# Stick-breaking prompt scores as 64-row products, two heads side by side, on one Trainium2 core

## The chip, the cores and the metric

The kernel runs on one core of a Trainium2 chip. The metric is the time of one execution on the device in microseconds (us), the median of several runs; lower is better. The engines are TensorE (matmuls and transposes; PE, its weight loads PEld), VectorE (DVE), ScalarE (ACT), GpSimd (POOL) and SyncE (SP, which issues the DMAs). They run at once, each through its own list of instructions in order, and wait for one another by semaphores.

## What is computed

Two layers of a hybrid encoder over 2048 prompt tokens and 8 x 16 sample tokens, width 1024: an input projection, a state-space branch, a stick-breaking attention branch of 8 heads of 64, and an output projection. The change touches the attention of the prompt alone:

```python
def stick_breaking(q, k, v, q_pos, k_pos):
    z = jnp.einsum('bqhd,bkhd->bhqk', q, k, preferred_element_type=jnp.float32) * (HEAD_DIM ** -0.5)
    mask = k_pos[None, :] < q_pos[:, None]
    log_1mb = jnp.where(mask, -jax.nn.softplus(z), 0.0)
    after = lax.cumsum(log_1mb, axis=3, reverse=True) - log_1mb
    a = jnp.where(mask, jnp.exp(jax.nn.log_sigmoid(z) + after), 0.0)
    return jnp.einsum('bhqk,bkhd->bqhd', a.astype(v.dtype), v)
```

## The kernel before

Q and K lie in DRAM transposed (`qT`, `kT`), each value split into a high part and a low part (`[512, 2, SEQ]`: 8 heads of 64 rows, two parts, tokens), since the matmuls take them at reduced precision.

`attn_prompt` (L778) runs over blocks of up to four query tiles of 128 tokens and over four pairs of heads (L782), then over key chunks of 512 tokens, the diagonal one first (L800), the two heads `hh` (L807) and the query tiles `i`. For one head, K's 64 rows of high and 64 of low parts fill all 128 rows of the array (`K1`); Q is loaded twice, as `Q1` in the same arrangement and as `Q2` with the parts exchanged. One score tile `pz` (128 queries x 512 keys, one PSUM bank) is then the sum of two products, L819 and L820, which hold all four combinations of parts. On the diagonal chunk the mask is added by a third product (L822), and a tile that needs less than 256 columns is computed at 256.

ScalarE turns `pz` into `u`, the sigmoid of minus the score (L824). VectorE multiplies `u` up from the right with a scan, in place (L826). TensorE transposes 128 columns of `u` of each query tile into `pt` (L836), VectorE copies the first head's `pt` to SBUF (L838) and ScalarE the second's (L839), and two products, one for each head on 64 of the array's columns, add `aT` times the differences of V into `po` (L842). At the end of a head pair VectorE adds a last term and multiplies by the gate (L851).

PSUM has eight banks. Until the last projection of layer 1 they are dealt out as two `m` (projections), two `z` (scores, but also parts of the state-space branch, of the sample attention and of the modulation), one `r` (`pr`: the transposes of the norm, L634, and of q and k, L696), two `t` and one `o`. After that, for the attention of layer 1, they are one `m`, three `z`, three `t` and one `o` (L109). Tiles with one tag take that tag's buffers in turn, in the order in which the program text asks for them.

The order on each engine is not the order of the program text: a scheduler puts ready instructions of later stages among those of earlier ones. In layer 0, the program text calls `attn_prompt(0)`, `glu(0)`, the modulation, `output(0, 0)` and then the projections of layer 1; on the engines these stages overlap.

Other lines that are spoken of: L673 to L675 and L726 to L728 (input projections), L1241 to L1243 (output projection), L1049 (transposes of 64 rows in the state-space branch), L242 (modulation, on 32 of the array's columns).

Of the kernel before, what the change touches and what calls it, by code (L numbers as in the profile page):

```python
# [8 lines left out]
F32 = mybir.dt.float32  # L9
F32R = mybir.dt.float32r  # L10
BF16 = mybir.dt.bfloat16
AF = mybir.ActivationFunctionType
# [32 lines left out]
class Trunk:  # L45
# [6 lines left out]
    def build(self):  # L52
        tc, nc = self.tc, self.nc
        with ExitStack() as es:
            self.dram = es.enter_context(tc.tile_pool(name="dram", bufs=1, space=DRAM))
            self.cp = self.pool(es, "const")
            self.pes = ExitStack()
            self.mb, self.zb, self.tb, self.ob = 2, 2, 2, 1
            self.ps = self.pes.enter_context(tc.tile_pool(name="ps", bufs=1, space=PSUM))
            self.scratch()  # L60
            self.consts()
            with ExitStack() as pe:
                with ExitStack() as px:
                    self.xp, self.xf = self.pool(px, "xp", right=True), []
                    self.rs0 = self.xp.tile([128, NT], F32, name="rs")
                    self.fetch(0)
                    self.fetch(1)
                    with ExitStack() as pv:
                        su = self.pool(pv, "sv", right=True)
                        self.mod(0, (2, 3, 0, 1))  # L70
                        self.ssm_params(su)
                    st = self.proj_open(pe, 0, 0)
                    with tc.high_priority(offset=300):
                        self.project(st, ("u",))
                self.project(st, ('q',))
                with ExitStack() as pq:
                    self.stats(self.pool(pq, "stats1", right=True), TILES[1])
                self.ssm_mats(0)
                with ExitStack() as ph:
                    self.ssm_phase(ph, 0)  # L80
                    self.ssm_phase(ph, 1)
                self.ssm_mats(1)
                self.ssm_sample(0)
                self.project(st, ('k', 'v', 'za', 'zs'))
                self.proj_half(st, 1)
                self.project(st, ("u",))
                self.ssm(0)
                self.attn_sample(0)
                self.project(st, ('zs', 'za', 'k', 'v', 'q'))
            self.attn_prompt(0, ((0, 4), (4, 4), (8, 4), (12, 4)))  # L90
            self.glu(0)
            self.mod(0, (4, 5), right=False)
            self.mod(1, (2, 3, 0, 1, 4, 5), right=False)
            self.output(0, 0)
            with ExitStack() as pe:
                st = self.proj_open(pe, 1, 0)
                self.project(st, ("u",))
                self.project(st, ('q', 'k', 'v', 'za', 'zs'))
            self.attn_sample(1)
            self.output(0, 1)  # L100
            with ExitStack() as pe:
                st = self.proj_open(pe, 1, 1)
                self.project(st, ("u",))
                self.ssm_sample(1)
                self.ssm(1)
                self.project(st, ('k', 'v', 'q', 'zs', 'za'))
            self.pes.close()
            self.ps = es.enter_context(tc.tile_pool(name="ps2", bufs=1, space=PSUM))
            self.mb, self.zb, self.tb, self.ob = 1, 3, 3, 1  # L109
            self.attn_prompt(1, ((0, 4), (4, 4), (8, 4)) + ((12, 2), (14, 2)))  # L110
            self.glu(1)
            self.output(1, 0)
            self.output(1, 1)
# [61 lines left out]
        return self.ps.tile([128, 512], F32, name="pm", tag="m", bufs=self.mb)  # L175

    def pr(self):
        return self.ps.tile([128, 512], F32, name="pr", tag="r", bufs=1)

    def po(self):  # L180
        return self.ps.tile([128, 512], F32, name="po", tag="o", bufs=self.ob)
# [595 lines left out]
    def attn_prompt(self, l, blocks):  # L777
        nc = self.nc  # L778
        v, gp, sc, pe, ident = nc.vector, nc.gpsimd, nc.scalar, nc.tensor, self.ident
        with ExitStack() as es:  # L780
            ap = self.pool(es, f"a{l}{blocks[0][0]}", right=True)
            for t0, nt, hp in [(t0, nt, hp) for t0, nt in blocks for hp in range(H // 2)]:  # L782
                nq = nt * 128
                qs = slice(t0 * 128, t0 * 128 + nq)
                rp = slice(hp * 128, (hp + 1) * 128)
                top = (t0 + nt - 1) // 4
                Qt = []
                for hh in range(2):
                    rs = slice(hp * 128 + hh * 64, hp * 128 + hh * 64 + 64)
                    Q1 = ap.tile([128, 512], F32R, name="Q1", bufs=3)  # L790
                    Q2 = ap.tile([128, 512], F32R, name="Q2", bufs=3)
                    self.dma(Q1[:, 0:nq], self.qT[l][rs, :, qs].rearrange("d s t -> (d s) t"))
                    self.dma(Q2[:, 0:nq], self.qT[l][rs, ::-1, qs])
                    Qt.append((Q1, Q2))
                po = self.po()
                vE = ap.tile([128, 4], F32, name="vE", bufs=2)
                with nc.allow_non_contiguous_dma(reason="layout"):
# [2 lines left out]
                for kc in range(top, -1, -1):  # L800
                    diag = kc == top
                    nk = (t0 + nt) * 128 - kc * 512 if diag else 512
                    ks = slice(kc * 512, kc * 512 + nk)
                    V1 = ap.tile([128, 4, 128], F32, name="V1", bufs=2)
                    self.dma(V1[:, 0:nk // 128], self.dv_d[l][ks, rp].rearrange("(b p) c -> p b c", p=128))
                    As = [[], []]
                    for hh in range(2):  # L807
                        rs = slice(hp * 128 + hh * 64, hp * 128 + hh * 64 + 64)
                        K1 = ap.tile([128, 512], F32R, name="K1", bufs=3)
                        self.dma(K1[:, 0:nk], self.kT[l][rs, :, ks].rearrange("d s t -> (d s) t"))  # L810
                        Q1, Q2 = Qt[hh]
                        for i in range(nt):
                            W = (t0 + i + 1) * 128 - kc * 512 if diag else 512
                            o = 512 - W
                            pz = self.pz()
                            qi = slice(i * 128, (i + 1) * 128)
                            N = max(W, 256)
                            c0, c1 = 512 - N, 512 - N + W
                            pe.matmul(pz[:, c0:512], Q1[:, qi], K1[:, 0:N], start=True, stop=False)  # L819
                            pe.matmul(pz[:, c0:512], Q2[:, qi], K1[:, 0:N], start=False, stop=not diag)  # L820
                            if diag:
                                pe.matmul(pz[:, c1 - 128:c1], self.identb, self.maskb, start=False, stop=True)  # L822
                            u = ap.tile([128, 512], F32, name="u", bufs=16)
                            sc.activation(u[:, o:512], pz[:, c0:c1], AF.Sigmoid, scale=-0.125)  # L824
                            un = u[:, o:512][:, ::-1]
                            v.tensor_tensor_scan(un, un, un, 1.0 if diag else carry[hh * 4 + i], ALU.mult, ALU.bypass)  # L826
                            carry[hh * 4 + i] = u[:, o:o + 1]
                            As[hh].append(u)
                    for j in range(nk // 128):
                        i0 = max(0, kc * 4 + j - t0)  # L830
                        s = slice(i0 * 128, nq)
                        pTs = [self.pt(), self.pt()]
                        for hh in range(2):
                            for i in range(i0, nt):
                                off = (512 - ((t0 + i + 1) * 128 - kc * 512)) if diag else 0
                                pe.transpose(pTs[hh][:, i * 128:(i + 1) * 128], As[hh][i][:, off + j * 128:off + (j + 1) * 128], ident)  # L836
                        aTs = [ap.tile([128, 512], F32, name="aT", bufs=4) for _ in range(2)]
                        v.tensor_copy(aTs[0][:, s], pTs[0][:, s])  # L838
                        last = sc.copy(aTs[1][:, s], pTs[1][:, s])  # L839
                        for hh in range(2):  # L840
                            c = slice(hh * 64, hh * 64 + 64)
                            mm = pe.matmul(po[c, s], V1[:, j, c], aTs[hh][:, s], start=diag and j == 0,  # L842
                                           stop=kc == 0 and j == 3, tile_position=(0, hh * 64))
                            if hh == 0:
                                self.after(mm, last)
# [436 lines left out]
```

## Time and profile before

| | |
|---|---|
| median of 3 runs | 3268.61 us (3263.9 to 3268.92) |
| the profiled execution | 3266.1 us, span 3264.3 us |
| VectorE busy | 2228.8 us |
| ScalarE busy | 1297.2 us |
| chain that ended last | TensorE 24%, VectorE 3% of the span, the rest under 2% each |
| score products L819 | from 1031.7 to 3212.5 us |

All times that are worked out stand beside the profiled execution's 3266.1 us. A matmul's duration in the profile includes a tail in which the next one already runs, so what a matmul holds of TensorE is read from the starts of neighbours, in the timeline.

### The profile page before, as it was taken

The numbers are of one execution on the slowest core, as the hardware profiler recorded it, in microseconds if no ns is written. First come the engines' busy times: TensorE is split into PE (matmuls) and PEld (weight loads), VectorE is DVE, ScalarE is ACT, GpSimd is POOL, SyncE is SP. The second block draws the span as 40 slices with busy tenths as digits, with TensorE's granted clock in tenths as the row PEclk, the third lists the DMA queues.
The fourth block names the chain that finished last, engine by engine and source line by source line (L and its number), as shares of the span: only waits on it lengthen the run. The fifth ranks groups of instructions, "written<-read, shape, count | busy, mean of one in ns | idle before, by whom it ended". The sixth has DMA issues, their size and how long they took to land. (4 is left out here: it accounts for less than half of the span.)

```text
span 3264.3 us, 47172 instructions
## 1 busy us (share of the span) xinstructions
PE 3019.6 (93%) x16902; PEld 2241.4 (69%) x16902; DVE 2228.8 (68%) x3885; ACT 1297.2 (40%) x2646; POOL 715.0 (22%) x468
## 2 busy tenths in 40 slices
PE   6978679899998999999999999989999899999998
PEld 4756577798767667667777785757789565666665
DVE  6699785667466776677895534376583989776865
ACT  5622225334342343465443324263343345343422
POOL 1155663102211022211021002222200202111210
PEclk8989899999999999999999999999999899999999
DMA  6645654565776974343344237437853846444642
GB/s 208 164 141 176 215 166 150 146 192 167 258 241 216 315 218 151 121 139 117 113 150 153 88 104 268 142 99 216 268 177 119 259 129 200 141 128 136 203 140 73
DMA packets 516100, 555.28 MB, mean 170 GB/s; under 512 B 87203, under 2 KB 369491, under 8 KB 515098
## 3 DMA queue, kind: packets, MB, share of 16 engines
q1 hardware_dynamic: 515866, 552.26, 53.9%
q8 instruction: 134, 2.20, 0.3%
q14 instruction: 100, 0.82, 0.1%
HBM read 378.12 MB, written 169.86 MB: 168 GB/s over the span
## 5 line engine op out<-in xcount | busy, mean ns | idle before, releaser
L826 DVE TENSOR_TENSOR_SCAN u<-u 128x512 f32<-128x512 f32 (+3 forms) x640 | 722.2, 1162 | 94.2 <-ACT u L824 90.7
L673 PE MATMUL pm<-wH,hH 128*128 128x512 f32 x1088 | 448.9, 414 | 38.4 <-ACT kn L760 18.9
L675 PE MATMUL pm<-wH,hL 128*128 128x512 f32 x1088 | 446.2, 410 | 10.6 <-POOL hL L649 6.0
L674 PE MATMUL pm<-wL,hH 128*128 128x512 f32 x1088 | 444.0, 408 | 9.9 <-DVE wL L172 8.0
L839 ACT COPY aT<-pt 128x512 f32<-128x512 f32 (+1 forms) x376 | 174.9, 469 | 595.3 <-PE pt L836 569.1
L836 PEld LDWEIGHTS pt<-ident,u 128*128 128x128 f32 x2176 | 242.1, 142 | 230.8 <-issue 194.1
L824 ACT ACTIVATE u<-pz 128x512 f32<-128x512 f32 (+3 forms) x640 | 320.7, 535 | 177.1 <-PE pz L822 61.3
L838 DVE COPY aT<-pt 128x512 f32<-128x512 f32 (+1 forms) x376 | 199.4, 533 | 253.8 <-PE pt L836 242.3
L836 PE MATMUL pt<-ident,u 128*128 128x128 f32 x2176 | 352.0, 285 | 12.9 <-DVE aT L838 9.3
L842 PE MATMUL po<-aT,V 128*64 128x512 f32 (+1 forms) x1504 | 317.7, 505 | 16.0 <-DVE aT L838 8.1
L819 PE MATMUL pz<-K,Q 128*128 128x512 f32 (+2 forms) x640 | 272.9, 427 | 6.1 <-ACT u L824 1.8
L726 PE MATMUL pm<-hH,wH 128*128 128x384 f32 (+1 forms) x768 | 258.9, 337 | 18.4 <-DVE kn L731 18.4
L673 PEld LDWEIGHTS pm<-wH,hH 128*128 128x128 f32 x1088 | 210.0, 193 | 90.2 <-ACT kn L760 20.4
L728 PE MATMUL pm<-hH,wL 128*128 128x384 f32 (+1 forms) x768 | 257.4, 336 | 10.2 <-POOL wL L172 10.2
L172 POOL TENSOR_TENSOR wL<-wr,wH 128x512 fp32r<-128x512 f32 x96 | 152.1, 1595 | 498.2 <-ACT wH L171 326.8
L727 PE MATMUL pm<-hL,wH 128*128 128x384 f32 (+1 forms) x768 | 257.8, 336 | 0.0
L675 PEld LDWEIGHTS pm<-wH,hL 128*128 128x128 f32 x1088 | 210.2, 193 | 66.2 <-POOL hL L649 10.6
L674 PEld LDWEIGHTS pm<-wL,hH 128*128 128x128 f32 x1088 | 210.2, 193 | 58.8 <-DVE wL L172 11.3
L820 PE MATMUL pz<-K,Q 128*128 128x512 f32 (+2 forms) x640 | 236.3, 370 | 0.0
L1241 PE MATMUL pm<-owH,mH 128*128 128x512 f32 x512 | 205.0, 402 | 2.1 <-ACT mH L171 1.2
L1242 PE MATMUL pm<-owL,mH 128*128 128x512 f32 x512 | 204.1, 399 | 3.1 <-DVE owL L172 3.1
L1243 PE MATMUL pm<-owH,mL 128*128 128x512 f32 x512 | 202.4, 396 | 0.0
(373 smaller groups left out, 5252.0 us busy)
## 6 DMA issues: line engine op xcount, KB each, us to landing
wr<-in_w_in_dram SPq DMA_DIRECT2D x192, 256.0 KB
K<-kT SPq DMA_DIRECT2D x184, 256.0 KB
Q<-qT SPq DMA_DIRECT2D x112, 256.0 KB
wm<-in_w_mod_dram SPq DMA_DIRECT2D x24, 1024.0 KB
V<-dv_d SPq DMA_DIRECT2D x92, 256.0 KB
out_dram<-kn SPq DMA_DIRECT2D x68, 256.0 KB
qT<-x SPq DMA_DIRECT2D x64, 256.0 KB
kT<-x SPq DMA_DIRECT2D x64, 256.0 KB
```

The costliest lines, as they stand in the source:

```text
L673: pe.matmul(ps, hH[:, k, cs], wH[k], start=k == 0, stop=False)
L674: pe.matmul(ps, hH[:, k, cs], wL[k], start=False, stop=False)
L675: pe.matmul(ps, hL[:, k, cs], wH[k], start=False, stop=k == KT - 1)
L726: pe.matmul(ps[:, 0:n], wH[k][:, ws], hH[:, k, 0:n], start=k == 0, stop=False)
L727: pe.matmul(ps[:, 0:n], wH[k][:, ws], hL[:, k, 0:n], start=False, stop=False)
L728: pe.matmul(ps[:, 0:n], wL[k][:, ws], hH[:, k, 0:n], start=False, stop=k == KT - 1)
L819: pe.matmul(pz[:, c0:512], Q1[:, qi], K1[:, 0:N], start=True, stop=False)
L820: pe.matmul(pz[:, c0:512], Q2[:, qi], K1[:, 0:N], start=False, stop=not diag)
L824: sc.activation(u[:, o:512], pz[:, c0:c1], AF.Sigmoid, scale=-0.125)
L826: v.tensor_tensor_scan(un, un, un, 1.0 if diag else carry[hh * 4 + i], ALU.mult, ALU.bypass)
L836: pe.transpose(pTs[hh][:, i * 128:(i + 1) * 128], As[hh][i][:, off + j * 128:off + (j + 1) * 128], ident)
L842: mm = pe.matmul(po[c, s], V1[:, j, c], aTs[hh][:, s], start=diag and j == 0, stop=kc == 0 and j == 3, tile_position=(0, hh * 64))
```

## The change

Q and K are now loaded once for both heads, with head 0 in rows 0 to 63 and head 1 in rows 64 to 127 and the two parts side by side (`Q`, `K`, 128 x 2 x 512). A score tile is the sum of three products of 64 rows: high by high, low by high, high by low; low by low is left out. The products of the two heads alternate, each on its 64 rows of the array (`tile_position=(hh * 64, 0)`), into two `pz` tiles. The first of the six also waits for an earlier sigmoid, so that both tiles are free. The tag `r` is gone: `pr` takes its buffers from the tag `z`, which has three instead of two.

```diff
-            self.mb, self.zb, self.tb, self.ob = 2, 2, 2, 1
+            self.mb, self.zb, self.tb, self.ob = 2, 3, 2, 1
...
     def pr(self):
-        return self.ps.tile([128, 512], F32, name="pr", tag="r", bufs=1)
+        return self.ps.tile([128, 512], F32, name="pr", tag="z", bufs=self.zb)
...
+            free = []
...
-                Qt = []
-                for hh in range(2):
-                    rs = slice(hp * 128 + hh * 64, hp * 128 + hh * 64 + 64)
-                    Q1 = ap.tile([128, 512], F32R, name="Q1", bufs=3)
-                    Q2 = ap.tile([128, 512], F32R, name="Q2", bufs=3)
-                    self.dma(Q1[:, 0:nq], self.qT[l][rs, :, qs].rearrange("d s t -> (d s) t"))
-                    self.dma(Q2[:, 0:nq], self.qT[l][rs, ::-1, qs])
-                    Qt.append((Q1, Q2))
+                Q = ap.tile([128, 2, 512], F32R, name="Q", bufs=2)
+                self.dma(Q[:, :, 0:nq], self.qT[l][rp, :, qs])
...
+                    K = ap.tile([128, 2, 512], F32R, name="K", bufs=3)
+                    self.dma(K[:, :, 0:nk], self.kT[l][rp, :, ks])
                     As = [[], []]
-                    for hh in range(2):
-                        rs = slice(hp * 128 + hh * 64, hp * 128 + hh * 64 + 64)
-                        K1 = ap.tile([128, 512], F32R, name="K1", bufs=3)
-                        self.dma(K1[:, 0:nk], self.kT[l][rs, :, ks].rearrange("d s t -> (d s) t"))
-                        Q1, Q2 = Qt[hh]
-                        for i in range(nt):
...
-                            pe.matmul(pz[:, c0:512], Q1[:, qi], K1[:, 0:N], start=True, stop=False)
-                            pe.matmul(pz[:, c0:512], Q2[:, qi], K1[:, 0:N], start=False, stop=not diag)
+                    for i in range(nt):
...
+                        pzs = [self.pz(), self.pz()]
+                        for n, (a, b) in enumerate(((0, 0), (1, 0), (0, 1))):
+                            for hh in range(2):
+                                r = slice(hh * 64, hh * 64 + 64)
+                                mm = pe.matmul(pzs[hh][:, c0:512], Q[r, a, qi], K[r, b, 0:N], start=n == 0,
+                                               stop=n == 2 and not diag, tile_position=(hh * 64, 0))
+                                if n == 0 and hh == 0 and len(free) >= self.zb - 1:
+                                    self.after(mm, free[1 - self.zb])
+                        for hh in range(2):
+                            pz = pzs[hh]
...
-                            sc.activation(u[:, o:512], pz[:, c0:c1], AF.Sigmoid, scale=-0.125)
+                            free.append(sc.activation(u[:, o:512], pz[:, c0:c1], AF.Sigmoid, scale=-0.125))
```

In the changed kernel the lines of `attn_prompt` below the products stand one higher: L814 is a score product, L821 the mask, L835 a transpose, L841 a value product.

The scheduler makes another order of the whole program from it. The first place is TensorE's list late in layer 0's attention before: score products beside transposes (L836), value products (L842) and the first norm transposes of layer 1 (L634).

```order
L819 MATMUL pz<-K_11510,Q_11383 128x512 [waits Activation_49]
L820 MATMUL pz<-K_11510,Q_11384 128x512
L819 MATMUL pz<-K_11510,Q_11383 128x512 [waits Activation_49]
L820 MATMUL pz<-K_11510,Q_11384 128x512
L836 MATMUL pt<-ident,u 128x128 [waits DVE_49]
L836 MATMUL pt<-ident,u 128x128 x2
L836 MATMUL pt<-ident,u 128x128 [waits Activation_49]
L836 MATMUL pt<-ident,u 128x128 x2
L634 MATMUL pr<-ident,x_15654 128x128 [waits Activation_49]
L634 MATMUL pr<-ident,x_15654 128x128 x3
```

Scores, transposes of `u` and the norm's transposes all use the whole array here, and the first norm of layer 1 stands among scores of layer 0; more of these follow behind it.

The second place is TensorE's list in the changed kernel at the end of layer 0's scores.

```order
L841 MATMUL po<-aT,V_13952 64x512 [waits DMAHW5_49,Activation_49]
L841 MATMUL po<-aT,V_13952 64x512
L835 MATMUL pt<-ident,u 128x128 [waits PE_49]
L835 MATMUL pt<-ident,u 128x128 x3
L814 MATMUL pz<-K,Q 128x512 [waits Activation_49]
L814 MATMUL pz<-K,Q 128x512 x5
L634 MATMUL pr<-ident,x_15798 128x128 [waits Activation_49]
L634 MATMUL pr<-ident,x_15798 128x128 x3
L835 MATMUL pt<-ident,u 128x128 [waits DVE_49]
L835 MATMUL pt<-ident,u 128x128 x3
```

The six products L814 stand between rows of the whole array, and the L634 shown is the first one of layer 1: it follows the last score group of layer 0. Ahead of it, back to the last output projection, the list holds only rows like these.

## Rows read from the trace of the kernel before

**Rows 1.** Page, busy time, share of the span and instructions of each engine.

```profile
PE 3019.6 (93%) x16902; PEld 2241.4 (69%) x16902; DVE 2228.8 (68%) x3885; ACT 1297.2 (40%) x2646; POOL 715.0 (22%) x468
```

**Rows 2.** Stretches: us, busy of PE, PEld, DVE, ACT, POOL; PEclk, DMA, GB/s.

```profile
1600.00:1900.00 300.00, 297.83 (x1560) 218.72 (x1559) 210.17 (x353) 120.24 (x223) 50.61 (x33) 1.00 0.38 123
...
2700.00:2800.00 100.00, 95.25 (x504) 60.04 (x502) 87.38 (x101) 49.00 (x99) 23.88 (x14) 0.98 0.68 204
...
2224.00:2475.00 251.00, 246.28 (x1298) 204.81 (x1298) 176.89 (x420) 102.93 (x207) 41.95 (x32) 1.00 0.66 201
```

**Rows 3.** Groups by line and shape, attention: busy us, mean ns | idle before.

```profile
L819 PE MATMUL pz<-K,Q 128*128 128x512 f32 x448 | 200.5, 447 | 3.2 <-DMA K<-kT 1.7 <-ACT u L824 1.4
...
L819 PE MATMUL pz<-K,Q 128*128 128x384 f32 x64 | 26.7, 417 | 0.0
...
L819 PE MATMUL pz<-K,Q 128*128 128x256 f32 x128 | 45.8, 358 | 2.9 <-issue 1.6 <-DVE kn L731 0.9 <-ACT u L824 0.4
...
L826 DVE TENSOR_TENSOR_SCAN u<-u 128x512 f32<-128x512 f32 x448 | 587.4, 1341 | 62.6 <-ACT u L824 59.8
...
L838 DVE COPY aT<-pt 128x512 f32<-128x512 f32 x172 | 117.6, 684 | 156.8 <-PE pt L836 155.3 <-PE po L842 0.7
...
L842 PE MATMUL po<-aT,V 128*64 128x256 f32 x560 | 90.9, 408 | 11.2 <-DVE aT L838 8.1 <-issue 2.9 <-DVE za L851 0.2
...
L851 DVE SCALAR_TENSOR_TENSOR za<-po,vE,za 128x128 f32<-128x128 f32 x126 | 35.2, 337 | 11.1 <-PE po L842 10.9
```

**Rows 4.** Timeline of PE and PEld near 3102 us: start, us, engine, line.

```profile
3101.45 0.48 PE L819 MATMUL pz<-K,Q 128*128 128x512 f32 x1
3101.77 0.39 PE L820 MATMUL pz<-K,Q 128*128 128x512 f32 x1
3102.00 0.38 PE L836 MATMUL pt<-ident,u 128*128 128x128 f32 x2
3102.31 0.65 PE L842 MATMUL po<-aT,V 128*64 128x256 f32 x4
3102.89 0.44 PE L836 MATMUL pt<-ident,u 128*128 128x128 f32 x2
...
3101.53 0.19 PEld L820 LDWEIGHTS pz<-K,Q 128*128 128x128 f32 x1
```

**Rows 5.** Timeline of PE and PEld near 2315 us; last, one L1049 load by shape.

```profile
2314.47 0.40 PE L675 MATMUL pm<-wH,hL 128*128 128x512 f32 x1
2314.80 1.21 PE L1049 MATMUL pt<-ident,y 64*128 64x64 f32 x16
2315.93 0.50 PE L673 MATMUL pm<-wH,hH 128*128 128x512 f32 x1
2316.27 0.40 PE L674 MATMUL pm<-wL,hH 128*128 128x512 f32 x1
...
2315.47 0.39 PEld L1049 LDWEIGHTS pt<-ident,y 64*128 64x128 f32 x5
...
L1049 PEld LDWEIGHTS pt<-ident,y 64*128 64x128 f32 x256 | 17.1, 139 | 4.7 <-issue 3.0 <-DVE xs L1010 0.6 <-ACT wH L171 0.4
```

**Rows 6.** L824 by shape; L836's durations (ns, min/median/max) by its line.

```profile
L824 ACT ACTIVATE u<-pz 128x512 f32<-128x512 f32 x448 | 250.5, 599 | 117.3 <-PE pz L820 60.7 <-PE pt L836 35.6 <-PE pz L822 15.3
...
L836 PE MATMUL pt<-ident,u x2176: 270/273/476, 1035.2 to 3249.0; 128*128 128x128 f32 x198
```

**Rows 7.** Who waited for whom, PE: us in total, times, longest us.

```profile
PE pr L696 <- DVE x L707: 18.8, 7, 10.6
...
PE pr L634 <- ACT x L639: 6.0, 6, 2.5
...
PE pz L819 <- ACT u L824: 1.8, 4, 1.2
...
PE pz L819 <- DMA K<-kT: 1.7, 1, 1.7
```

More of the change, by code (lines that the diff above doesn't have):

```diff
@@ L805, in attn_prompt @@
                     self.dma(V1[:, 0:nk // 128], self.dv_d[l][ks, rp].rearrange("(b p) c -> p b c", p=128))
+                    K = ap.tile([128, 2, 512], F32R, name="K", bufs=3)
+                    self.dma(K[:, :, 0:nk], self.kT[l][rp, :, ks])
                     As = [[], []]
-                    for hh in range(2):
-                        rs = slice(hp * 128 + hh * 64, hp * 128 + hh * 64 + 64)
-                        K1 = ap.tile([128, 512], F32R, name="K1", bufs=3)
-                        self.dma(K1[:, 0:nk], self.kT[l][rs, :, ks].rearrange("d s t -> (d s) t"))
-                        Q1, Q2 = Qt[hh]
-                        for i in range(nt):
[L813 to L818, printed above, removed]
-                            pe.matmul(pz[:, c0:512], Q1[:, qi], K1[:, 0:N], start=True, stop=False)
-                            pe.matmul(pz[:, c0:512], Q2[:, qi], K1[:, 0:N], start=False, stop=not diag)
+                    for i in range(nt):
+                        W = (t0 + i + 1) * 128 - kc * 512 if diag else 512
+                        o = 512 - W
+                        qi = slice(i * 128, (i + 1) * 128)
+                        N = max(W, 256)
+                        c0, c1 = 512 - N, 512 - N + W
+                        pzs = [self.pz(), self.pz()]
[8 more added lines that the diff above has]
+                            pz = pzs[hh]
                             if diag:
```

## The prediction, made before the changed kernel ran

> **What bounds the kernel now.** I read the page's busy times first. TensorE is busy 93% of the 3264.3 us span, VectorE 68% [rows 1], so the average points at TensorE. Then the same by stretch, since the change touches only the attention on the prompt: late in layer 0's attention TensorE is busy 297.83 of 300 us, VectorE 210.17; in layer 1's attention 95.25 and 87.38 of 100 [rows 2]. TensorE sets the pace in both, but only because the scheduler mixes attention with projections. Attention alone asks more of VectorE: a scan of 512 columns takes 1341 ns and there are two for each query tile and head pair, and one copy of 684 ns for every 128 keys of the four query tiles of a block [rows 3]. So two questions decide: what the new score products cost TensorE, and whether the mixing survives.
>
> **The products saved.** A 512-column score product holds TensorE 0.23 us (from L820's start at 3101.77 to the next at 3102.00) [rows 4]; its busy time of some 0.4 us includes a tail that the next product overlaps. Per head pair and query tile there were four products; now there are three steps of two 64-row products each. If the two of a step run side by side, one step of 0.23 us is saved. By the counts of L819 [rows 3], two heads together: 224 x 0.23 + 32 x 0.17 + 64 x 0.12 = 52 + 5 + 8 = 65 us (the narrower steps scaled by columns). That two products side by side do run at the price of one is shown on the column halves: four L842 products of 256 columns begin and end in 0.65 us [rows 4], where one alone is busy 408 ns [rows 3]. Bounds: 65 us saved, or, if nothing overlaps, 130 us lost (six steps for four); I take the saving, by that nearest row.
> The Trainium skill, "TensorE: Matmul & The Clock Gate", Part 3, gives 3.07 times for four row tiles of 512 columns, 77% of ideal; by that a step would be an estimated 0.30 us and the sum 47 us worse. No run here shows row tiles side by side yet.
>
> **The change of array shape.** All score products used the full array, like the transposes and projections around them. Now a group of six stands in 64-row tiles, between others in the full array. Before shows what such an excursion costs: L1049's transposes use 64 rows. From L675's start at 2314.47 to L674's at 2316.27 is 1.80 us [rows 5]. In it stand L675 and L673 (0.23 each) and 16 transposes, whose step is 0.062 us: five weight loads span 0.39, one is 139 ns, so (0.39 - 0.14) / 4. That makes 1.45; 0.35 us is over, 0.175 a change of shape. Part is a pause (L675 holds 0.33 rather than 0.23), part the first weight load, which no product hides (L673 holds 0.34). Counted along TensorE's whole list, changes of shape go from 990 to 1667: 677 more, at 0.175 us 118 us. Bounds: 0.10 us each if the first load hides, 0.20 if two loads at the start stand one behind the other; 68 to 135 us. So the rearranged products cost 118 - 65 = 53 us more than they save. A fifth of the groups (64 of 320, layer 0's last block) go to the stretch below, so this term is 43 us.
>
> **The shared PSUM ring.** `pr` (projection transposes) now takes its buffers in turn with `pz`. In the order of before, layer 1's first norm transposes stand among layer 0's scores; now the first stands behind the very last score. Between the last output projection and that row lie 62 score groups, nearly the whole last block, with nothing beside them but transposes and value products. VectorE's work there, for one head pair: three full key chunks of 8 scans and 4 copies, 3 x (8 x 1.34 + 4 x 0.68) = 40.4 us; the diagonal one, whose widths add up to 2.5 times 512 columns, 2.5 x (2 x 1.34 + 0.68) = 8.4 us; four closings of 0.34 [rows 3]: 50.2 us, 201 for four pairs. TensorE's for the same in before: scores 13.6, 116 transposes of 0.11, value products about 15 with their changes of shape (0.58 for 256 columns, twice the stream about 1.0 for 512) [rows 4, 6]: 43 us, 172 in all, and there it was the bound. At the 87% to 100% that VectorE could reach (87.38 of 100 is the highest row in attention), the stretch takes 201 to 231 us; I take 90%, 223: 51 us lost. Bounds 29 and 59 by this arithmetic; 0 if the order runs better mixed than it reads.
> The same ring pulls apart the sample attention of layer 0 from the q and k projections behind it, and layer 1's state-space scan from its k and q. Each has some 400 rows with few neighbours now; before, TensorE was busy 246.28 of 251 us around the latter, VectorE 176.89 [rows 2]. At the same share lost (51 of 223) of some 110 us, my estimate for 400 rows of 0.11 to 0.23 and the like: 25 us, bounds 0 and 70.
>
> **What gets better, and the added wait.** `pr` had one buffer. TensorE's waits for its release total 18.8 and 6.0 us [rows 7]; two more buffers may remove them: between 0 and -25, I take -14 us, since VectorE's queue, which ends the larger, is late anyway. The first product of a group now waits for the first sigmoid of the group ahead; queued behind it are all later TensorE instructions. A 512-column sigmoid takes 599 ns [rows 6], about 0.8 us from the last product. In the new order 24 of 319 groups come within 1 us of the one ahead, by the steps above: at most 24 x 0.8 = 19 us, probably 4 us; score products lost 1.8 us in such waits before [rows 7]. Q's loads fall to a quarter in number and K's to half on SP's queue; K's bytes are the same, Q's halve. TensorE lost 1.7 us waiting for K [rows 7], so this is 0, and without that cover those 1.7 us.
>
> **Sum.** 43 + 51 + 25 - 14 + 4 = 109 us on the profiled execution's 3266.1 us: 3375 us. That execution lies 2.5 us under the median shown and inside the three runs.
>
> **Rivals.**
> *The mixing is not lost* (0.2): TensorE stays the bound in the long stretch since its own waits shrink. The ring terms fall away, all 53 us of shape changes count, less 10: 3309. For it: TensorE was 95.25 busy where VectorE was 87.38 [rows 2]. Against: 50 us of VectorE stand to 43 of TensorE.
> *Weight loads are no longer hidden inside a group* (0.13). In before it is hidden: L820's load runs from 3101.53 for 0.19 us, while L819 works in the same rows [rows 4]. If the loads of steps two and three wait for their own rows, each exposes what L673 shows after a change, 0.11 us: 320 x 2 x 0.11 = 70, less the fifth that VectorE covers, 56: 3431.
> The Trainium skill, "TensorE: Matmul & The Clock Gate", Part 3, "The mechanism", says that a load overlaps running products only when the row group differs; by that rule this rival would hold. The trace of full-array products disagrees with it.
> *The row tiles do not run side by side* (0.06): six steps, 195 us from the first term, less a fifth, on top: 3531.
> *Faster* (0.08): the shape change is nearly free for these groups, the mechanism of the opposite sign. It decides at 65 / 677 = 0.096 us a change if nothing else were lost. At 0.03 us (20 us), with 20 us of lost mixing and all 25 of `pr`'s waits gone: 3266 - 65 + 20 + 20 - 25 = 3216. Against it are both excursions seen: the column tiles also pause, two transposes of 0.11 and the pause filling 0.31 us ahead of L842 [rows 4, 6].
> *No change* (0.03): the same at 0.08 us a change.
>
> **How the numbers follow.** The forecast has 0.5. The range 3290 to 3445 takes in the first two rivals and the bounds of the ring terms; outside are the faster and unchanged cases, the serial one and a few per cent of tails. Its own case spans 3330 to 3420. About 0.2% (6.5 us) is what a measurement of this kernel can tell from no change: faster 0.08, within 0.04, slower 0.88.
>
> **What would show it.** Steps: L814 in pairs that start together, three steps of 0.23 us a group. Shape: about 0.1 us pause ahead of a group and behind it. Ring: a stretch of some 220 us without projections, VectorE near 90% and TensorE clearly under its 99%, then projections with VectorE idle. Right for the wrong reason would be products of a group 0.2 us apart each. I am wrong if layer 0's attention stays TensorE-bound, or if the pauses are missing.

## The result, and the profile after

The changed kernel is slower: 3635.03 us median of four runs (3631.12 to 3641.03), beside 3266.26 for the kernel before on the same chip. The ratio is 1.1134, with a 95% interval of 1.111 to 1.1159: 369 us more. The forecast was 3375 us, with a range up to 3445: the sign is right, the size is wrong by more than a factor of three (369 against 109).

The page of the changed kernel: busy times, then TensorE's share and clock in 40 slices of the 3639.2 us span.

```profile
PE 3122.9 (86%) x17542; PEld 2227.6 (61%) x17542; DVE 2203.7 (61%) x3885; ACT 1301.3 (36%) x2646; POOL 693.8 (19%) x468
...
PE   6960369999788999999999999894589899999999
...
PEclk8985589999898999999999999897799899999999
```

TensorE is now busy 86% of the span instead of 93% [rows 1]. Its busy time grew by 103 us, the span by 375: most of the loss is a TensorE that stands or runs slowly, and it does so in two places that hold few or no prompt scores, slices 3 to 6 (182 to 546 us) and slices 28 and 29 (2456 to 2638 us).

I divide both programs at layer 0's first score product, its last, and layer 1's first and last. Windows of the changed kernel (us, busy of PE, PEld, DVE, ACT, POOL, clock, DMA, GB/s), first up to the first score, then layer 0's scores, then up to layer 1's, then layer 1's:

```profile
0.00:1164.00 1164.00, 856.75 (x4824) 687.88 (x4824) 668.01 (x1460) 390.39 (x783) 312.49 (x212) 0.86 0.50 156
1164.00:1834.00 670.00, 641.50 (x3935) 382.80 (x3936) 521.82 (x672) 279.78 (x555) 84.12 (x44) 0.96 0.48 150
1834.00:2875.00 1041.00, 899.93 (x4690) 720.22 (x4686) 458.06 (x1045) 344.82 (x685) 177.36 (x142) 0.92 0.45 144
2875.00:3591.00 716.00, 683.38 (x3874) 409.71 (x3874) 538.32 (x679) 277.30 (x601) 114.28 (x66) 0.97 0.47 146
```

The same four in the kernel before:

```profile
0.00:1032.00 1032.00, 882.77 (x5008) 712.10 (x5008) 726.31 (x1493) 395.92 (x798) 341.24 (x217) 0.95 0.60 187
1032.00:1887.00 855.00, 838.37 (x4719) 588.22 (x4719) 602.78 (x987) 373.77 (x733) 131.38 (x82) 0.99 0.49 157
1887.00:2524.00 637.00, 602.52 (x3406) 476.52 (x3404) 338.41 (x697) 241.74 (x491) 123.38 (x99) 0.98 0.56 176
2524.00:3212.00 688.00, 651.85 (x3548) 436.12 (x3546) 543.27 (x676) 275.86 (x599) 113.50 (x66) 0.98 0.54 164
```

Read them as three stages: **setup** 1032 to 1164 (+132); **middle**, layer 0's scores and what follows up to layer 1's, 1492 to 1711 (+219); **layer 1's attention** 688 to 716 (+28); the end after it -4. That is the 375 us. Of the three, only the last turns out to come from the score products alone (table of stages below).

**The setup.** In it the program makes two sets of state-space matrices: L497 transposes the input `Cn` of a set, L573 the matrices `GG`, and L563 is the product of each matrix step. (In the edited kernels further down, line numbers differ by a few.) Who TensorE waited for between 200 and 600 us, changed kernel (us in total, times, longest):

```profile
PE pt L497 <- DMA Cn<-in_ssm_c_im_dram: 85.5, 1, 85.5
PE pz L563 <- POOL EE L552: 36.0, 8, 6.5
PE pt L573 <- DVE GG L557: 23.1, 5, 7.6
```

and its windows, the changed kernel's ahead of the one of before:

```profile
200.00:600.00 400.00, 183.82 (x883) 133.86 (x882) 278.27 (x419) 73.81 (x122) 186.78 (x102) 0.68 0.42 131
```

```profile
200.00:600.00 400.00, 317.11 (x1596) 259.05 (x1590) 320.38 (x460) 131.64 (x245) 214.30 (x117) 0.93 0.53 168
```

TensorE's busy time falls by 133 us in 400, which is the stage's loss. It is not the DMA that is slow: `Cn` is loaded for the second set of state-space matrices, and its load is issued at 362 us in the changed kernel and at 418 in the one before. What differs is what TensorE has meanwhile. In the numbered order of TensorE's list (neighbours of one kind as one row), the first set's last product L563 is row 652 in the changed kernel and the second set's first transpose row 653:

```
651 L563 MATMUL pz_2309<-EE_2298,Bb1_1982 32x256 x3
652 L563 MATMUL pz_2309<-EE_2298,Bz_2039 32x256
653 L497 MATMUL pt_2491<-ident_96,Cn_2483 128x128 x4
```

In the kernel before they are rows 668 and 1159, with 490 rows of projections between, those of k among them. The program text asks for the projections of k after both sets (`ssm_mats(1)`, `ssm_sample(0)`, then `project` of k, v, za, zs). Each k tile needs a `pr`, each matrix step a `pz`. With a ring in common, a `pr` that is asked for later can't get its buffer before the earlier `pz` have been through theirs, so k's transposes can't run ahead any more, and with them goes the work that filled TensorE while VectorE and GpSimd make the matrices.

**The score products.** Timeline of TensorE in layer 1's attention, changed kernel (start, duration, then line and count), and the weight loads of the same group:

```profile
3453.59 0.66 PE L835 MATMUL pt<-ident,u 128*128 128x128 f32 x4
3454.17 0.97 PE L814 MATMUL pz<-K,Q 64*128 64x512 f32 x6
3455.07 0.65 PE L841 MATMUL po<-aT,V 128*64 128x256 f32 x4
```

```profile
3454.17 0.54 PEld L814 LDWEIGHTS pz<-K,Q 64*128 64x128 f32 x6 [0.17 <-ACT aT L838]
```

Six products in 0.97 us: pairs start 3 ns apart at 3454.17, 3454.52 and 3454.75, and L841 follows at 3455.07. The steps are 0.34 (its first load is exposed), 0.24 and 0.32 (with the way out). So the two heads run side by side at the price of one, and the loads of the second and third step hide. Of 960 pairs 932 start within 25 ns of each other.

### The profile page after: what moved, and what is told of

Read it like the earlier page. It is cut to its first block, busy times and chain, and to the rows that moved or that the text cites. A ratio compares the mean times of both kernels' runs of the same rounds, so it can differ in the third digit from the quotient of the medians.

```text
span 3639.2 us, 48146 instructions
## 1 busy us (share of the span) xinstructions
PE 3122.9 (86%) x17542; PEld 2227.6 (61%) x17542; DVE 2203.7 (61%) x3885; ACT 1301.3 (36%) x2646; POOL 693.8 (19%) x468
## 5 line engine op out<-in xcount | busy, mean ns | idle before, releaser
L835 PEld LDWEIGHTS pt<-ident,u 128*128 128x128 f32 x2176 | 240.7, 143 | 314.7 <-issue 243.4
L835 PE MATMUL pt<-ident,u 128*128 128x128 f32 x2176 | 386.1, 292 | 34.4 <-DVE aT L837 19.6
L823 ACT ACTIVATE u<-pz 128x512 f32<-128x512 f32 (+3 forms) x640 | 307.8, 531 | 278.3 <-PE pz L814 160.9
L841 PE MATMUL po<-aT,V 128*64 128x512 f32 (+1 forms) x1504 | 323.4, 510 | 13.0 <-DVE aT L837 6.6
L814 PE MATMUL pz<-K,Q 64*128 64x512 f32 (+2 forms) x1920 | 304.7, 411 | 4.1 <-ACT u L823 2.9
L172 DVE TENSOR_TENSOR wL<-wr,wH 128x512 fp32r<-128x512 f32 x96 | 104.7, 1099 | 182.8 <-ACT wH L171 180.3
L814 PEld LDWEIGHTS pz<-K,Q 64*128 64x128 f32 x1920 | 160.5, 191 | 89.2 <-issue 58.0
L172 POOL TENSOR_TENSOR wL<-wr,wH 128x512 fp32r<-128x512 f32 x96 | 143.3, 1504 | 375.3 <-ACT wH L171 136.4
```

The costliest lines, as they stand in the source:

```text
L814: mm = pe.matmul(pzs[hh][:, c0:512], Q[r, a, qi], K[r, b, 0:N], start=n == 0, stop=n == 2 and not diag, tile_position=(hh * 64, 0))
L823: free.append(sc.activation(u[:, o:512], pz[:, c0:c1], AF.Sigmoid, scale=-0.125))
```

## The experiments

All kernels here compute the whole result. The medians were taken beside the kernel before on the same chip; "+n" is against that. First the change's two halves, then the reach of the ring, then the parts that were open. The expectations name runs by label: e1_own_ring, e2_ring_only and e3_rows_layer1 are experiments 1 to 3; e11 and e12 are 4 and 5; e9 is 6; e5 and e6 are 7 and 8; e4 is 9; e10 is 10; e7 and e8 are 11 and 12.

**1. The 64-row products with `pr` in a bank of its own** (changed kernel):

```diff
-            self.mb, self.zb, self.tb, self.ob = 2, 3, 2, 1
+            self.mb, self.zb, self.tb, self.ob = 2, 2, 2, 1
...
-        return self.ps.tile([128, 512], F32, name="pr", tag="z", bufs=self.zb)
+        return self.ps.tile([128, 512], F32, name="pr", tag="r", bufs=1)
```

> The change, but pr has its own buffer again (tag r, one buffer) and z has two buffers until the last projection; a score group waits for the second sigmoid of the group ahead. Theory (the shared ring costs most of the 369 us; the 64-row products cost only their changes of array shape): TensorE's list has 752 changes of shape more than before, at 0.175 us 132 us, less 65 us of products saved: 3266 + 67 = 3333 us (3300 to 3360). Rival (the 64-row groups themselves, their waits for sigmoids and their pairing cost most of it): above 3500 us.

Measured 3344.2 us, 1.0264 [1.0247, 1.0282]: +83.

**2. The shared ring alone** (kernel before, the reverse edit, score products as they were):

> The kernel before, with full-array products and two loads of Q, but pr takes its buffers from z, which has three. Theory (shared ring): the 369 us less the some 55 us of the score products, so 3266 + 314 = 3580 us (3530 to 3620), with TensorE at half clock and under half busy between 250 and 500 us. Rival (the score products cost most): under 3330 us.

Measured 3609.18 us, 1.1069 [1.1044, 1.1093]: +348. The ring alone makes nearly the whole loss. The halves add up to 431, more than 369. The surplus lies in the middle (57 + 210 against 219 in the table of stages below); that changes of shape cost little where TensorE waits anyway would explain it, but no run shows that by itself. Its setup is the changed kernel's:

```profile
PE pt L497 <- DMA Cn<-in_ssm_c_im_dram: 85.4, 1, 85.4
```

**3. 64-row products in layer 1's attention only** (kernel before; there the banks are dealt out anew and no `pr` exists; `attn_prompt_rows` is the changed `attn_prompt`):

```diff
-            self.attn_prompt(1, ((0, 4), (4, 4), (8, 4)) + ((12, 2), (14, 2)))
+            self.attn_prompt_rows(1, ((0, 4), (4, 4), (8, 4)) + ((12, 2), (14, 2)))
```

> The kernel before for layer 0, its rings too; the 64-row groups with one Q and one K load in layer 1's attention alone, where z has three buffers in both kernels and pr is not used. 356 changes of shape more than before, at 0.175 us 62 us, less 32 us of products saved: 3266 + 30 = 3296 us (3280 to 3310). If a change of shape cost nothing: 3234 us. If the wait for the sigmoid of the group ahead were dear in layer 1: over 3330 us.

Measured 3290.27 us, 1.0097 [1.0074, 1.0119]: +29. Half of the 65 us of saved products lies here, and TensorE's list has 356 changes of shape more than before: (29 + 32) / 356 = 0.17 us each. In experiment 1 it is (83 + 65) / 752 = 0.20. Both figures take the saving as worked out and put all the rest down to the changes. The group at 3454.17 shows most of that price directly: about 0.09 us of pause ahead of it, 0.11 more in its first step and 0.09 more in its last, 0.29 us for one way in and one way out, without what the next shape's first load may add.

**4. The ring in layer 1 only, and 5. in layer 0 only** (kernel before; `pr` from tag `z` with its two buffers for one layer, from `r` for the other):

```diff
-    def pr(self):
+    def pr(self, l):
+        if l == 1:
+            return self.ps.tile([128, 512], F32, name="pr", tag="z", bufs=self.zb)
         return self.ps.tile([128, 512], F32, name="pr", tag="r", bufs=1)
```

> The kernel before (full-array products), but layer 1's pr takes its buffers from z, which keeps its two; layer 0's pr has its own. Theory (the order of the turns, by stage): from e2_ring_only's trace, where layer 0's first score to layer 1's first score takes 210 us longer than before: 3261 + 210 = 3470 us (3430 to 3510), with layer 0's first score at 1032 us as before. If the number of buffers rather than their order counted, two for both kinds would be dearer than e2's three: above 3520 us.

> The kernel before, but layer 0's pr takes its buffers from z, which keeps its two; layer 1's pr has its own. Theory: layer 0's first score comes 125 us later, as in e2_ring_only, and the rest is as before: 3261 + 125 = 3386 us (3360 to 3420).

Measured 3404.82 us, 1.044 [1.0418, 1.0461], +145, for layer 1; 3475.24, 1.0657 [1.064, 1.0673], +215, for layer 0. Together 360, about the 348 of the whole ring. But both lie outside the ranges expected: layer 0's share is larger, layer 1's smaller. Two buffers in common instead of experiment 2's three cost 23 us more in the setup (148 against 125) and nothing that shows in the middle (62 + 141 against 210), so the number of buffers is not the main thing. The setup tells them apart, layer 1 first:

```profile
200.00:600.00 400.00, 314.60 (x1586) 258.22 (x1585) 319.34 (x458) 131.37 (x247) 215.35 (x117) 0.93 0.52 167
```

```profile
200.00:600.00 400.00, 180.14 (x869) 131.02 (x868) 267.29 (x401) 72.52 (x120) 174.57 (x101) 0.68 0.41 131
...
PE pt L499 <- DMA Cn<-in_ssm_c_im_dram: 87.3, 1, 87.3
```

The second has the wait of 87.3 us and its first score at 1180 us instead of 1032; the first has neither.

**6. The attention left alone, without a ring** (kernel before; layer 1's first norm transpose waits for layer 0's last sigmoid):

```diff
+                    if l == 1 and half == 0 and li == 0 and q == 0 and j == 0:
+                        self.after(mm, self.sig)
...
-                            sc.activation(u[:, o:512], pz[:, c0:c1], AF.Sigmoid, scale=-0.125)
+                            self.sig = sc.activation(u[:, o:512], pz[:, c0:c1], AF.Sigmoid, scale=-0.125)
```

> The kernel before with its own rings, but the first norm transpose of layer 1's first half also waits for the last score sigmoid of layer 0, so that no projection of layer 1 stands beside layer 0's attention; nothing else differs. It measures the lost mixing by itself. The prediction's working: 51 us, 3312 us. The comparison of e5_ring_k_first with e6_own_ring_k_first says more: attention of layer 0 678 instead of 855 us, while some 295 us of projection products move behind it, so 118 us: 3380 us.

Measured 3300.71 us, 1.0144 [1.0115, 1.0173]: +45. The prediction's 51 us is near; the 118 us that I had drawn from experiments 7 and 8 is far off. It is also the control for experiment 4. In both, layer 0's scores end at 1628 us; these are the windows from there to layer 1's first score, here and in experiment 4:

```profile
1628.00:2560.00 932.00, 874.55 (x4691) 701.84 (x4690) 462.26 (x1045) 342.28 (x685) 183.00 (x142) 0.98 0.50 160
```

```profile
1628.00:2662.00 1034.00, 893.19 (x4686) 717.06 (x4685) 461.88 (x1045) 344.92 (x685) 180.36 (x142) 0.93 0.45 144
...
PE pz L1036 <- DMA Hi<-HT: 29.4, 4, 15.3
PE po L1146 <- DVE HS L1133: 21.1, 1, 21.1
PE pt L973 <- DMA uj<-u_d: 15.9, 2, 13.7
```

The same instructions (4691 and 4686, VectorE 462 us in both) take 102 us more under the ring. The waits listed, 66 us, are in layer 1's state-space scans, of the samples (L1146) and of the prompt (L973, L1036), which ask for `pz` between projections that ask for `pr`. In experiment 6 TensorE loses nothing to `Hi<-HT`, nothing to L1146 and only this to `u_d` in its window:

```profile
PE pt L973 <- DMA uj<-u_d: 0.9, 1, 0.9
```

**7. The ring with k asked for earlier** (kernel of experiment 2, program text moved; **8.** is the same move without the ring):

```diff
-                self.project(st, ('q',))
+                self.project(st, ('q', 'k'))
...
-                self.project(st, ('k', 'v', 'za', 'zs'))
+                self.project(st, ('v', 'za', 'zs'))
...
-                self.project(st, ("u",))
+                self.project(st, ("u", 'k', 'q'))
                 self.ssm_sample(1)
                 self.ssm(1)
-                self.project(st, ('k', 'v', 'q', 'zs', 'za'))
+                self.project(st, ('v', 'zs', 'za'))
```

> As e2_ring_only (full-array products, pr in z's ring of three), but the program text asks for layer 0's k projection before the state-space matrices, and for k and q of layer 1's second half before its state-space stages. Theory (buffers of one tag are handed out in the order of the program text, so pr of k waits behind all pz of those stages, and TensorE stands without projections): most of the 348 us of e2_ring_only comes back, 3609 - 250 = 3360 us (3310 to 3420); what is left is layer 0's attention without projections. Rival (it is the sharing itself, too few buffers for both kinds at once): stays above 3540 us.

> The same two moves in the kernel before, with pr's own buffer: a control. Theory: the order of the text does not matter to separate rings, the scheduler mixes the stages either way: 3261 us within 15. Rival (the moves gain by themselves): under 3235 us, and then e5's gain says less about the ring.

Measured 3436.03 us, 1.0531 [1.0513, 1.0549], +173, with the ring; 3280.06, 1.0047 [1.0031, 1.0063], +17, without. Half the ring's loss comes back by the order of the requests alone, though less than I expected (3310 to 3420); the control, too, is 2 us outside its 15. The setup is nearly whole again:

```profile
200.00:600.00 400.00, 299.88 (x1486) 245.78 (x1487) 294.34 (x449) 115.76 (x206) 205.85 (x113) 0.87 0.50 163
```

and the first score stands at 1049 us instead of 1157. The middle stays long: 1679 us against 1492 before and 1526 in experiment 8. So the order of the requests is shown as the cause in the setup, while in the middle, set against experiment 8, it gave back 57 of 210 us: 187 - 34 = 153 are left. That only v and the gates are left to stand beside layer 1's scan, once k and q are pulled ahead of it, may be the reason; no run shows it.

**9. The six products in another order** (kernel of experiment 1, all three of one head, then of the other):

```diff
-                        for n, (a, b) in enumerate(((0, 0), (1, 0), (0, 1))):
-                            for hh in range(2):
+                        for hh in range(2):
+                            for n, (a, b) in enumerate(((0, 0), (1, 0), (0, 1))):
```

> As e1_own_ring, but the three products of one head come before the three of the other, so that neighbours mostly use the same 64 rows. If two row tiles run side by side only when they alternate (theory): each group takes up to six steps of 0.23 us instead of three, 3 x 0.23 x 224 + 3 x 0.17 x 32 + 3 x 0.12 x 64 = 194 us more than e1_own_ring. If a group's products never ran side by side, or if those of the second head start while the first's run: the same time as e1_own_ring.

Measured 3360.61 us, 1.0315 [1.0293, 1.0338]: 16 more than experiment 1, where I expected some 190. Timeline of TensorE, first a whole group, then one that the scheduler had split:

```profile
3012.53 0.97 PE L814 MATMUL pz<-K,Q 64*128 64x512 f32 x6
```

```profile
1547.65 0.97 PE L814 MATMUL pz<-K,Q 64*128 64x512 f32 x3
1548.55 0.33 PE L835 MATMUL pt<-ident,u 128*128 128x128 f32 x1
1548.80 0.97 PE L814 MATMUL pz<-K,Q 64*128 64x512 f32 x3
```

Six products issued three and three still take 0.97 us, as long as three of one head do alone. So the alternating order isn't what pairs them; that both heads follow each other without other work between is. 829 of 960 pairs start together.

**10. Without the added wait** (kernel of experiment 1, the lines with `free[1 - self.zb]` removed):

> As e1_own_ring, without the added wait of a group's first product for a sigmoid of the group ahead; each tile's own first product then waits for its buffer. 139 changes of shape more than e1, since groups are split more often, 24 us at 0.175; less at most 11 us, which TensorE's loads lost waiting for sigmoids in e1. Theory (the added wait is cheap and keeps groups whole): 3344 + 15 = 3360 us. Rival (the wait is a main cost of e1's 83 us): under 3320 us.

Measured 3415.01 us, 1.0496 [1.0471, 1.0522]: 71 more than experiment 1, or 76 with each set against its own run of the kernel before. The wait, booked as a cost of 4 us, earns that. Without it the scheduler puts other work into the groups: 139 more changes of shape, and 523 of 960 pairs start together instead of 916. In its timeline three products of one head now take as long as six did:

```profile
3007.25 0.97 PE L814 MATMUL pz<-K,Q 64*128 64x512 f32 x3
3008.15 0.65 PE L839 MATMUL po<-aT,V 128*64 128x256 f32 x4
3008.73 0.44 PE L833 MATMUL pt<-ident,u 128*128 128x128 f32 x2
3009.10 0.95 PE L814 MATMUL pz<-K,Q 64*128 64x512 f32 x3
```

**11. Four score banks in layer 1, and 12. twelve products in a row** (kernel of experiment 3 with one `pt` bank given to `pz`; then two query tiles' products in one group, so that 123 changes of shape go):

```diff
-            self.mb, self.zb, self.tb, self.ob = 1, 3, 3, 1
+            self.mb, self.zb, self.tb, self.ob = 1, 4, 2, 1
```

> As e3_rows_layer1, with z four and t two in layer 1, a control for e8. 31 changes of shape less than e3: 5 us less, and up to 15 us more for the transposes' third buffer: 3285 to 3305 us.

> As e7, but the 64-row products of two query tiles stand together, twelve in a row, ahead of their sigmoids, so that two groups share an entry and an exit; 123 changes of shape less than e7. Theory (0.175 us a change): e7 less 22 us. If the cost of the 64-row groups lay in something else (slower steps, waits for sigmoids): as e7, or slower, since the first of twelve waits for the last sigmoid of the twelve ahead.

Measured 3329.36 us, 1.0199 [1.0177, 1.0221], +66, and 3336.18, 1.0212 [1.0189, 1.0236], +73. Both missed: giving the third `pt` bank to `pz` cost 37 us (66 - 29), and the larger group gave nothing. TensorE's waits behind 2500 us, number 11 and then number 12:

```profile
PE pt L914 <- DVE aT L916: 17.0, 17, 2.5
...
PE po L920 <- ACT aT L917: 13.2, 38, 1.7
```

```profile
PE pt L919 <- DVE aT L921: 26.5, 27, 5.7
PE po L925 <- ACT aT L922: 25.3, 50, 2.9
```

The 123 changes at 0.17 us would have given 21 us back; these two waits alone take 22 (51.8 against 30.2). As a second price for a change of shape the pair is inconclusive.

No kernel here was faster than the one before.

## Why the prediction was wrong in size

The stages of the profiled executions, in us (before: 1032, 1492, 688):

| kernel | setup | middle | layer 1's attention |
|---|---|---|---|
| changed | +132 | +219 | +28 |
| products alone (exp. 1) | 0 | +57 | +30 |
| ring alone (2) | +125 | +210 | -5 |
| ring in layer 1 (4) | -3 | +141 | 0 |
| ring in layer 0 (5) | +148 | +62 | -3 |
| attention alone (6) | -2 | +38 | -7 |
| ring, k first (7) | +17 | +187 | -33 |
| k first, no ring (8) | +8 | +34 | -26 |

**The failed step** is the last paragraph of "The shared PSUM ring": "The same ring pulls apart the sample attention of layer 0 from the q and k projections behind it, and layer 1's state-space scan from its k and q", priced at 25 us with 70 as the upper bound. It failed twice.

- It was mis-sized in the middle. The part in layer 1 measures 102 us (experiment 4 against 6, the same work in 1034 and 932 us). I took the loss of mixing that I had worked out for the attention, where TensorE's and VectorE's work are nearly equal, 172 and 201 us, and carried its share (51 of 223) to some 110 us of rows. But in the scan the wait is for a chain of transfers and VectorE steps (`HT`, `HS`, `u_d`), not for a busy engine. VectorE was busy 462 of those 1034 us. The wait showed where the ring kept other work away from the scan (experiment 6 has hardly any of it), and its length can't be had from busy shares. How much of the 102 us is the order of the requests stays open: moving k and q ahead brought back a part (experiment 7).
- It left out the setup, +125 us with the ring alone. There k's `pr` come behind the `pz` of both sets of state-space matrices. I read the new order at the places where attention stands and not at every place where both tags are asked for. (The sample attention that I did name also lies in the setup, but TensorE's busy time between 200 and 600 us, the stretch of the matrices, falls by 133 us, as much as the stage lost.) Its knock-on is the 62 us that layer 0's ring leaves in the middle. Some 180 TensorE instructions that the setup no longer holds stand there, and 47 of the 62 us are TensorE's busy time; experiment 5, then the kernel before:

```profile
1180.00:2734.00 1554.00, 1487.67 (x8302) 1099.11 (x8301) 991.46 (x1716) 623.60 (x1239) 272.74 (x186) 0.98 0.52 166
```

```profile
1032.00:2524.00 1492.00, 1440.89 (x8123) 1064.74 (x8122) 941.19 (x1683) 615.52 (x1224) 254.76 (x181) 0.99 0.52 165
```

Those three add up: setup 125, middle 62 + 102 + 38 (attention alone) = 202 of the measured 210.

**What held.**

- *The attention alone, 51 us.* In the changed kernel the stretch without projections is this window:

```profile
1623.00:1834.00 211.00, 199.04 (x1171) 100.65 (x1171) 193.96 (x256) 110.39 (x209) 9.29 (x5) 0.95 0.31 95
```

  It takes 211 us where 223 were forecast, VectorE busy 194 of them (92%, forecast 90%); experiment 6 gives 45 us for it. TensorE is less clearly free than I wrote, 94% by its modelled ends against 99% [rows 2]; its one longer wait there is for VectorE's copies `aT` (11 us), as a stretch paced by VectorE would have it.
- *Shape changes and saved products, 53 us.* Measured alone +83 in experiment 1 (752 changes rather than 677) and +29 for layer 1. At 0.17 to 0.20 us a change, the 0.175 read from one excursion [rows 5] is borne out, and with it the sign of this half: the changes of shape cost more than the saved products give. That figure is a remainder; the group at 3454.17, with 0.29 us for one way in and one way out, supports it, and experiments 11 and 12 give no second one.
- *The side-by-side step and the hidden loads.* Both as forecast; the rivals that rest on their failing (3431 and 3531 us) fall. The Trainium skill, "TensorE: Matmul & The Clock Gate", Part 3, "The mechanism", has a line by which a load overlaps running products only when the row group differs; the paragraph ahead of that line also lets a load into the background weight buffer run ahead. The group at 3454.17 does not bear out the line: the loads for the third step run beside the second step's products in the same rows (all six loads lie between 3454.17 and 3454.71), and the second step takes 0.24 us.
- *The rival "the mixing is not lost"* falls too: the windows without projections show it lost in three places.
- *The pair's wait* was wrong in sign (experiment 10), *`pr`'s released waits* (-14 us) are not seen: the waits at `pr` were 18.8 and 6.0 us before [rows 7] and are 28.3 us at L696 (now for `kn`) and 11.9 at L634 in the changed kernel. No wait for *K or Q loads* is among the changed kernel's eleven longest, as booked.
- *Two sums of the prediction* are off without moving the forecast. The three terms named for TensorE's work of one head pair add up to 41 us, not 43 (the mask products are not named). And "the same at 0.08 us a change" comes to 3250 us by its own terms, not to no change; that would take some 0.10 us.

So of the 109 us forecast, 94 (51 + 43) stood in terms that hold, and 25 in a term that measures 125 + 62 + 102.

## What to carry to other kernels

In this program a PSUM tag is also an order: whoever shares one is served in the order of the program text, and the scheduler can no longer move the later user ahead. Before merging two tags, list every place in the program where one asks behind the other, and ask what runs beside the waiting chain there; the costliest place need not be near the edit. Two products side by side in half the rows saved 0.23 us a group here and paid some 0.17 us for each way in and each way out. By that sum longer runs would turn it round, but no run shows it: the twelve products of experiment 12 gave nothing.

## What the runs showed of the hardware that I had not expected

- Products on different row tiles pair up even when they are issued one head after the other (experiment 9: 0.97 us for six, and 0.97 for three alone).
- The way into a 64-row group is a pause of about 0.09 us (the last L835 starts at 3453.97, takes a step of 0.11, L814 starts at 3454.17) and an exposed load of 0.11. The Trainium skill, "TensorEngine Tiling (Array Packing)", "Key Properties", says that a change of tiling mode drains TensorE; the pause agrees, and here it has a price.
- TensorE also lost its clock while it waited here, so waits cost more than their length. In the setup windows above the granted clock is 0.68 on average, before 0.93. Behind a wait of 5.18 us it is 0.50, the lower of the two levels (1.2 GHz), and from one product to the next it takes 0.43 us instead of 0.23 [rows 4].

```profile
232.60:234.80 2.20, 2.20 (x7) 1.75 (x6) 2.20 (x3) 0.66 (x2) 2.20 (x2) 0.50 0.00 0
...
230.96 1.94 PE L573 MATMUL pt<-ident,GG 128*128 128x128 f32 x8 [5.18 <-DVE rsm L197]
...
233.55 0.63 PE L675 MATMUL pm<-wH,hL 128*128 128x512 f32 x1
233.98 0.63 PE L673 MATMUL pm<-wH,hH 128*128 128x512 f32 x1
```
